# Differential attention on one core: the squares of the turned output go in front of two casts in ScalarE's order

## The chip, the cores and the metric

The kernel is one launch on one core of a Trainium2 chip. Its engines are TensorE (PE in the profile, with PEld for its weight loads), VectorE (DVE), ScalarE (ACT), GpSimd (POOL) and SyncE (SP, which here only starts DMAs). Each engine works through its own list of instructions in order, and engines wait for each other on semaphores. The metric is the device time of one execution in microseconds (us): the median of the runs.

## What is computed

One layer of a hybrid backbone for 256 prompt tokens and 2048 latent tokens. The part that the change touches is the differential attention and the norm behind it:

```python
def diff_attention(q, k, v, lam):
    ...
        s = jnp.einsum('bqhmd,bkhmd->bhmqk', qblk, k).astype(jnp.float32) * scale
        p = jax.nn.softmax(s, axis=-1)
        a = p[:, :, 0] - lam * p[:, :, 1]
        return jnp.einsum('bhqk,bkhe->bqhe', a.astype(v.dtype), v)

def merge(attn, four, subln_g, lam_init, w_out):
    b, n = attn.shape[:2]
    a = rms_norm(attn, subln_g) * (1.0 - lam_init)
    return jnp.concatenate([a.reshape(b, n, ATTN_WIDTH), four], axis=-1) @ w_out
```

There are 4 heads with 2 softmax maps each. A latent query sees 512 cached keys and 2048 latent keys, 2560 in all. The output of a head (128 wide) is normed by its own mean square: that is what the squares are for.

## The kernel before, in words

**Stages.** First the input projection with the Fourier mixing, then attention (about 518 to 1281 us of the span, from the first scores to the last squares), then the output projection and the two products of the MLP.

**A group.** Attention runs over 4 heads of 8 groups (class `Group`, g = 0 to 7) of 256 latent queries, so 32 groups. A group takes four slots, one for each half j of 128 queries and each map m. For a slot, `fill` (L1081) computes the scores in 5 PSUM banks of 512 keys (tile S), `rowmax` (L1086, VectorE) finds the largest of each bank, `comb` (L1089, VectorE) the largest of all, and `exp` (L1105, ScalarE, with the sums) writes the exponentials to P0 or P1. The 5 banks S are all that there are, so the fill of the next slot's bank b waits for this slot's exp of bank b. `combine` (L1110 to L1121, mostly GpSimd) makes P0 - lambda' P1.

**The product with V, two slots behind.** The combined map is turned by transposes on TensorE, `tr(kb)` (L1136), two key blocks at a time into a PSUM tile pt, of which there are two. `ah(kb)` (L1143, ScalarE) copies pt to SBUF, as a cast to the high part; `al(kb)` (L1148, VectorE) takes the rest, pt minus the high part. For two of the ten pairs, kb = 4 and 14, the copy is exact and there is no low part. Only after that is a pt free for the next `tr`. `mul(kb)` multiplies with V into the bank po: L95, L96 and L97 for high and low parts, L1162 for the pairs 4 and 14. Slots alternate between two pairs and three: 0 and 2; 4, 6 and 8; 10 and 12; 14, 16 and 18. I number the slots of a group's own exps 0 to 3; the transposes of pairs 10 and 12 of the group ahead stand in slot 0, those of 14, 16 and 18 in slot 1.

**The end of a group.** When a group's products are complete, `o1` (L1173) copies po columns 0 to 255 to SBUF, `o2` (L1177) turns the two halves back into columns 256 to 511 of the same bank po, `o4` (L1183) squares these on ScalarE with a sum over each row, twice 128x128, and `o5` to `o9` turn the sums to a factor on GpSimd, send it through DRAM and scale the output. There is one po. The next group's products write its columns 0 to 255 while `o2` and `o4` use the other half, and TensorE's first matmul into po behind `o4` in the program, the next group's `mul(4)` (L1162), waits for the squares.

**What sets the order.** Each step is entered with a time, `add(t, fn)`, and the whole stage is written out in order of these times (L1363 to L1365), which fixes the order on every engine. T is the length of a slot in that table and u = T / 5. The times are only keys for sorting. For the last group (`gr.last`) the steps behind `o1` are kept in a list, LASTO, and called from the output projection in the order of that list.

Of the kernel before, what the change touches and what calls it, by code (L numbers as in the profile page):

```python
# [41 lines left out]
def body(tc, a, out):  # L42
    nc = tc.nc
    ctx = ExitStack()
    with ctx:
# [944 lines left out]
        with ExitStack() as c3_:  # L990
# [289 lines left out]
            def add(t, fn, *args):  # L1280
                ev.append((t, len(ev), fn, args))
# [20 lines left out]
            for h in range(H):  # L1302
                hd, hp = Head(0, h), Head(1, h)
                base = h * 32 * T
                add(base - 18 * T + 0.7 if h else -3.04 * T, hd.load_k)
                add(base - 14 * T + 0.7 if h else 0.9 * T, hd.load_v)
                e = 4 * T * (h == H - 1)
                add(base + 2 * T - e + 0.7, hp.load_k)
                add(base + 2 * T - e + 0.71, hp.load_v)
                gp = Prompt(hp, 0)  # L1310
                G = [base + (AVS + 4 * g) * T for g in range(8)]
                add(G[1] - 3 * T - e, gp.qload)
                for j in range(2):
                    for m in range(2):
                        for t, fn in ((0.4, gp.scores), (0.85, gp.rowmax), (2.7, gp.exp)):
                            add(G[1 + 2 * j + m] - e + t * u, fn, j, m)
                    add(G[2 + 2 * j] - e + 8 * u, gp.combine, j)
                for t, fn, *args in ((0.25, gp.tr, 0), (0.9, gp.ah), (1.4, gp.al), (17.0, gp.mul), (20.85, gp.o1), (24.45, gp.oq),
                                     (25.3, gp.o2), (26.0, gp.o5), (26.05, gp.opow), (29.5, gp.o6), (34.0, gp.o7),
                                     (40.2, gp.o8), (43.0, gp.o9)):  # L1320
                    add(G[5] - e + t * u, fn, *args)
                for g in range(hd.ng):
                    gr = Group(hd, g)
                    add(base - (4 if h or g > 1 else 3) * T + 0.6 * u if base else -3.03 * T, gr.qload)
                    for st in range(4):
                        j, m = divmod(st, 2)
                        t0 = base + st * T
                        for b in range(hd.nbk):
                            add(t0 - T + (0.76 + 0.66 * b) * u, gr.fill, j, m, b)
                            add(t0 - T + (1.26 + 0.66 * b) * u, gr.rowmax, j, m, b)  # L1330
                            add(t0 + 0.66 * b * u, gr.exp, j, m, b)
                        add(t0 - 0.45 * u, gr.comb, j, m)
                        if m:
                            add(t0 + (4.5 if gr.last and j else 5.9) * u, gr.combine, j)
                            if gr.last and j:
                                add(t0 + T + 5.3 * u, gr.combine_v, j)
                    kbs = list(range(0, hd.nkt, 2))
                    for q in range(4):
                        w = base + (AVS + q) * T
                        if q % 2 == 0:  # L1340
                            order = [kbs.pop(0) for _ in range(2)]
                            tr_t, ah_t, al_t = [0.7, 2.2], [3.3, 3.8], [4.6, 5.2]
                        else:
                            order = [kbs.pop(0) for _ in range(3)]
                            tr_t, ah_t, al_t = [0.7, 2.2, 3.86], [3.3, 3.8, 4.4], [None, 4.6, 5.2]
                        for n, kb in enumerate(order):
                            add(w + tr_t[n] * u, gr.tr, kb)
                            add(w + (2.0 if gr.drain and kb == FULL[0] else ah_t[n]) * u, gr.ah, kb)
                            if al_t[n]:
                                add(w + al_t[n] * u, gr.al, kb)  # L1350
                            add(w + T + (3.9 + 0.01 * n) * u, gr.mul, kb)
                            if q == 3 and not n:
                                add(w + 3.95 * u, gr.mul_part, kb)
                    w = base + (AVS + 5) * T + 1.0 * u
                    for t, fn in ((0, gr.o1), (0.4, gr.o2), (7.85, gr.o4), (9.2, gr.o5), (11.8, gr.o6), (16.3, gr.o7), (23.4, gr.o8), (26.0, gr.o9)):
                        if gr.last and t > 1:
                            LASTO.append(fn)
                        else:
                            add(w + t * u, fn)
                    base += 4 * T  # L1360
# [357 lines left out]
        with c5r, ExitStack() as c5:  # L1718
# [157 lines left out]
            with tc.manual_schedule():  # L1876
                for n, (q, p) in enumerate(ITEMS):
# [22 lines left out]
                    fn, args = FINISH.get(n, (None, ()))  # L1900
# [66 lines left out]
        with ExitStack() as c6:  # L1967
# [62 lines left out]
            with tc.manual_schedule():  # L2030
# [41 lines left out]
                for j in range(3):  # L2072
                    t = 6 + j
# [70 lines left out]
```

## Time and profile before

| | |
|---|---|
| median of 3 runs | 2888.55 us (2887.37 to 2888.84) |
| the profiled execution | 2891.27 us |
| its span | 2889.5 us |
| TensorE busy | 2831.2 us, 98% of the span |
| ScalarE busy | 1538.7 us, 53% |
| VectorE busy | 1977.9 us, 68% |
| GpSimd busy | 1075.5 us, 37% |
| mean granted clock of TensorE | 0.998 |

A row of the timeline gives the start in us, the length, the engine, the line, what is written from what, how often (x2 for two in a row, merged), and in brackets how long the engine had been idle and whose work ended that. A row of the waits gives who waited for whom, the total in us, the number of times and the longest. A matmul row's end is modelled. ScalarE's exps and squares with a sum appear as two rows, the activation and the reading of the accumulator; a row can begin a little before the one ahead of it has ended.

### The profile page before, as it was taken

How to read it: one execution, taken by the hardware profiler on the slowest of the kernel's cores; microseconds unless marked ns; L12 is line 12 of the kernel's file. 1: busy time of each engine (PE TensorE's matmuls, PEld its weight loads, DVE VectorE, ACT ScalarE, POOL GpSimd, SP SyncE). 2: the span in 40 equal slices, each digit the busy share in tenths (PEclk: the TensorE clock that was granted, in tenths of full speed). 3: DMA queues.
4: the chain of work that ended last, by engine and by line, in shares of the span. 5: the costliest groups of instructions: out<-in, count | busy, mean ns of one | idle time of the engine just before them, and what ended most of it. 6: DMA issues, size and time to landing. Idle time of an engine off the chain costs nothing.

```text
span 2889.5 us, 42978 instructions
## 1 busy us (share of the span) xinstructions
PE 2831.2 (98%) x15029; PEld 2452.5 (85%) x15029; DVE 1977.9 (68%) x3325; ACT 1538.7 (53%) x3479; POOL 1075.5 (37%) x887
## 2 busy tenths in 40 slices
PE   8999999999999999999999999999999999999999
PEld 5888888687788888788889999999998888888887
DVE  7767786887887888864468778777775344345554
ACT  4333333788888888863356566556554332232221
POOL 1211223788898898852213333334332000000000
PEclk9999999999999999999999999999999999999999
DMA  7777767331222321337776676676656464445663
GB/s 282 222 203 206 229 203 250 150 108 47 77 74 52 110 43 43 97 74 219 235 238 223 217 245 230 220 241 223 219 192 235 148 203 151 138 143 176 206 208 110
DMA packets 404795, 497.69 MB, mean 172 GB/s; under 512 B 31539, under 2 KB 320672, under 8 KB 401506
## 3 DMA queue, kind: packets, MB, share of 16 engines
q1 hardware_dynamic: 399088, 484.35, 53.0%
q0 software_dynamic: 1936, 7.41, 0.8%
q10 hardware_dynamic: 3554, 3.17, 0.3%
q8 instruction: 119, 1.95, 0.3%
q14 instruction: 98, 0.80, 0.1%
HBM read 317.30 MB, written 179.62 MB: 172 GB/s over the span
## 4 chain that ended last, share of the span: by engine, by line
PE 54%; DVE 1%; issue 0%; ACT 0%; POOL 0%; DVEq 0%
PE ps L95 8%; PE ps L97 8%; PE ps L96 8%; PE pB L1761 2%; PE pB L1760 2%; PE pB L1759 2%; PE pA L1760 2%; PE pC L1760 2%; PE pC L1759 2%; PE pA L1759 2%; PE pA L1761 2%; PE pC L1761 2%; PE po L97 2%; PE po L96 2%; PE po L95 2%; PE pD L1761 1%
## 5 line engine op out<-in xcount | busy, mean ns | idle before, releaser
L1086 DVE TENSOR_REDUCE mxs<-Ss 128x1 f32<-128x512 f32 x636 | 405.3, 686 | 125.9 <-PE Ss L1081 118.0
L1436 DVE TENSOR_TENSOR sl<-sr,sh 128x768 fp32r<-128x768 f32 x168 | 161.8, 964 | 331.5 <-ACT sh L1435 331.1
L1121 POOL TENSOR_TENSOR P0s<-P0s,P1s 128x1024 f32<-128x1024 f32 (+2 forms) x128 | 376.7, 2943 | 10.7
L1435 ACT CAST sh<-sr 128x768 fp32r<-128x768 f32 x168 | 140.6, 838 | 418.3 <-PE ps L96 418.3
L1801 POOL TENSOR_TENSOR gs<-g,g 128x384 f32<-128x384 f32 x48 | 69.7, 1453 | 469.3 <-ACT g L1771 426.4
L1105 ACT ACTIVATE P1s<-Ss,mxs 128x512 f32<-128x512 f32 x318 | 215.4, 694 | 37.9 <-DVE mxs L1089 37.3
L95 PE MATMUL pj<-wh,hh 128*128 128x512 f32 x576 | 228.6, 397 | 2.8 <-DVE hh L556 2.0
L95 PE MATMUL ps<-thT,sh 128*128 128x512 f32 x585 | 227.6, 389 | 0.0
L96 PE MATMUL ps<-tlT,sh 128*128 128x512 f32 x585 | 227.6, 389 | 0.0
L97 PE MATMUL ps<-thT,sl 128*128 128x512 f32 x585 | 227.6, 389 | 0.0
L96 PE MATMUL pj<-wl,hh 128*128 128x512 f32 x576 | 226.8, 394 | 0.5 <-DVE wl L517 0.5
L97 PE MATMUL pj<-wh,hl 128*128 128x512 f32 x576 | 225.3, 391 | 0.0
L1105 ACT ACTIVATE P0s<-Ss,mxs 128x512 f32<-128x512 f32 x318 | 214.5, 692 | 4.9 <-DVE mxs L1089 4.0
L1136 PE MATMUL pts<-ident,P0s 128*128 128x128 f32 x1280 | 192.3, 274 | 4.4 <-DVE als L1148 1.8
L1081 PE MATMUL Ss<-KS0s,Qs 128*128 128x512 f32 x636 | 190.4, 420 | 0.4 <-ACT P1s L1105 0.4
L1081 PE MATMUL Ss<-KS1s,Qs 128*128 128x512 f32 x636 | 189.3, 422 | 1.5 <-ACT P0s L1105 1.1
L1770 ACT ACTIVATE g<-uz 128x384 f32<-128x384 f32 x144 | 75.7, 526 | 200.7 <-DVE uz L1793 174.0
L1136 PEld LDWEIGHTS pts<-ident,P0s 128*128 128x128 f32 x1280 | 152.2, 140 | 35.8 <-issue 4.6
L1143 ACT CAST ahs<-pts 128x512 fp32r<-128x512 f32 x256 | 146.4, 606 | 60.4 <-PE pts L1136 60.4
L1120 POOL TENSOR_SCALAR P1s<-P1s,tots 128x1024 f32<-128x1024 f32 (+2 forms) x128 | 172.0, 1344 | 5.7
L1148 DVE TENSOR_TENSOR als<-pts,ahs 128x512 fp32r<-128x512 f32 x256 | 163.7, 681 | 12.0 <-ACT ahs L1143 11.9
L95 PE MATMUL ps<-ophT,sh 128*128 128x512 f32 x423 | 164.7, 389 | 1.1 <-DVE uz L1793 1.1
(534 smaller groups left out, 8020.0 us busy)
## 6 DMA issues: line engine op xcount, KB each, us to landing
sr<-sd SPq DMA_DIRECT2D x84, 768.0 KB, 4.3
a<-in_w SPq DMA_DIRECT2D x184, 256.0 KB, 3.6
sd<-gs SPq DMA_DIRECT2D x192, 192.0 KB, 1.9
sd<-g SPq DMA_DIRECT2D x144, 192.0 KB, 4.2
wm<-in_w_mod SPq DMA_DIRECT2D x32, 512.0 KB, 5.3
Qs<-qd SPq DMA_DIRECT2D x32, 512.0 KB, 5.3
b<-in_w SPq DMA_DIRECT2D x64, 256.0 KB, 4.8
b<-tsum SPq DMA_DIRECT2D x64, 256.0 KB, 4.6
```

Of the source, the lines that this page charges most:

```text
L95: nc.tensor.matmul(ps, lh, rh, start=first, stop=False)
L96: nc.tensor.matmul(ps, lh, rl, start=False, stop=False)
L97: nc.tensor.matmul(ps, ll, rh, start=False, stop=last)
L1081: nc.tensor.matmul(S[:, :w], self.Q[:, x, m, j * P:j * P + P], self.hd.KS[m][:, b * 512:b * 512 + w], start=(x == 0), stop=(x == 1))
L1086: nc.vector.tensor_reduce(self.mx[j][:, m, b:b + 1], self.S[j, m, b], axis=AX.X, op=ALU.max)
L1105: nc.scalar.activation(dst, S, AF.Exp, bias=self.mx[j][:, m, 6:7], accum_out=self.sm[j][:, m, b:b + 1])
L1120: nc.gpsimd.tensor_scalar(p, p, tot[:, 3:4], 0.0, op0=ALU.mult, op1=ALU.add)
L1121: nc.gpsimd.tensor_add(d, d, p)
L1136: nc.tensor.transpose(pt[:, c:c + P], self.p0[j][:, (kb + t) * P:(kb + t + 1) * P], ident)
L1759: nc.tensor.matmul(ps, wh[:, c], hh[:, k, :], start=first and k == 0, stop=False, skip_group_check=True)
L1760: nc.tensor.matmul(ps, wh[:, c], hl[:, k, :], start=False, stop=False, skip_group_check=True)
L1761: nc.tensor.matmul(ps, wl[:, c], hh[:, k, :], start=False, stop=k == 3, skip_group_check=True)
```

## The change

One number in the table of times: `o4`, the squares, is entered 0.95 u earlier, and so sorts in front of the casts of the same slot instead of behind them.

```diff
                     w = base + (AVS + 5) * T + 1.0 * u
-                    for t, fn in ((0, gr.o1), (0.4, gr.o2), (7.85, gr.o4), (9.2, gr.o5), (11.8, gr.o6), (16.3, gr.o7), (23.4, gr.o8), (26.0, gr.o9)):
+                    for t, fn in ((0, gr.o1), (0.4, gr.o2), (6.9, gr.o4), (9.2, gr.o5), (11.8, gr.o6), (16.3, gr.o7), (23.4, gr.o8), (26.0, gr.o9)):
                         if gr.last and t > 1:
                             LASTO.append(fn)
```

ScalarE's order in slot 0 of group 3 of the first head, as a difference (osqs_0 and osss_0 are the squares and their sums of group 0, ahs_1_10 the cast of pair 10 of group 1, P0s_3_0 and P1s_3_0 the exps of group 3; a number at the end of a name counts tiles):

```order
 L1105 ACTIVATE P0s_3_0_5902,sms_3_0_5841<-Ss_3_0_0_4_5874,mxs_3_0_5840 128x512
-L1143 CAST ahs_1_10_5947<-pts_1_10_5910 128x512
-L1143 CAST ahs_1_12_5952<-pts_1_12_5936 128x512
-L1183 ACTIVATE osqs_0_5954,osss_0_5955<-po 128x128 x2
+L1183 ACTIVATE osqs_0_5946,osss_0_5947<-po 128x128 x2
+L1143 CAST ahs_1_10_5951<-pts_1_10_5910 128x512
+L1143 CAST ahs_1_12_5956<-pts_1_12_5936 128x512
 L1105 ACTIVATE P1s_3_0_0_5976,sms_3_0_5841<-Ss_3_0_1_0_5915,mxs_3_0_5840 128x512
```

The two squares now stand directly behind the last exp of map 0, and the casts of pairs 10 and 12 behind them. This happens 31 times, once for each group but the last, whose `o4` is in LASTO.

The last of the 31 places has no exps around it, since there is no further group (group 6 and 7 of the last head):

```order
 L1143 CAST ahs_7_8_14724<-pts_7_8_14707 128x512
-L1143 CAST ahs_7_10_14742<-pts_7_10_14731 128x512
-L1143 CAST ahs_7_12_14744<-pts_7_12_14737 128x512
-L1183 ACTIVATE osqs_6_14746,osss_6_14747<-po 128x128 x2
+L1183 ACTIVATE osqs_6_14742,osss_6_14743<-po 128x128 x2
+L1143 CAST ahs_7_10_14746<-pts_7_10_14731 128x512
+L1143 CAST ahs_7_12_14748<-pts_7_12_14737 128x512
 L1143 COPY ahs_7_14_14781<-pts_7_14_14770 128x512
```

Here too the squares move past two casts. On TensorE, VectorE and GpSimd no instruction changes its place. On SyncE one does, at the end of attention (att_79 is the attention output of group 6 of the last head, xo are rows of x for the residual):

```order
 L1582 DMA mT_14900<-four 128x4x128
-L1208 DMA att_79<-oTs_6_14694 128x256
 L1576 DMA xo_14903<-in_x_prompt 128x1024
 L1576 DMA xo_14905<-in_x_sample 128x1024
+L1208 DMA att_79<-oTs_6_14694 128x256
 L217 DMA g_1_14865<-gate_104 128x1024
```

The store of that output now stands behind two loads of x.

## Prediction

> **What bounds the kernel now.** I read the page first, then the table of windows, then the waits of TensorE and ScalarE alone in the steady part of attention (583 to 1275 us), then the timeline of one group, engine by engine.
>
> ```profile
> span 2889.5 us, 42978 instructions
> PE 2831.2 (98%) x15029; PEld 2452.5 (85%) x15029; DVE 1977.9 (68%) x3325; ACT 1538.7 (53%) x3479; POOL 1075.5 (37%) x887
> ```
>
> TensorE is busy 98% of the span, so only time in which it stands still is to be had from a reordering: 2889.5 - 2831.2 = 58.3 us. The windows give length, then busy us of PE, PEld, DVE, ACT and POOL, TensorE's granted clock, DMA share and GB/s, here for a piece of attention and for the last stage:
>
> ```profile
> 583.00:700.00 117.00, 112.26 (x719) 94.56 (x718) 94.64 (x187) 101.11 (x284) 103.18 (x84) 1.00 0.27 77
> 2300.00:2880.00 580.00, 580.00 (x2561) 480.41 (x2560) 279.18 (x370) 161.98 (x223) 0.00 (x0) 1.00 0.50 166
> ```
>
> In attention TensorE is idle 4.74 of 117 us, in the last stage not at all, at the same clock of 1.00. What ends its idle time in attention is one row, and the largest waits of ScalarE there are two:
>
> ```profile
> PE po L1162 <- ACT osqs L1183: 28.1, 31, 1.4
> ...
> ACT ahs L1143 <- PE pts L1136: 60.7, 91, 3.1
> ACT P1s L1105 <- DVE mxs L1089: 33.8, 56, 1.5
> ```
>
> TensorE waits 28.1 us, 31 times, for the squares; ScalarE waits 60.7 us for TensorE's transposes and 33.8 us for VectorE's row maximum. TensorE sets the pace, but for a stop once in each group. The stop itself, on TensorE:
>
> ```profile
> 605.03 1.19 PE L1081 MATMUL Ss<-KS1s,Qs 128*128 128x512 f32 x4
> 607.09 1.13 PE L1162 MATMUL po<-ahs,vf4s 128*128 128x256 f32 x4 [0.86 <-ACT osqs L1183]
> 609.45 0.60 PE L1136 MATMUL pts<-ident,P0s 128*128 128x128 f32 x4
> ...
> 611.62 1.17 PE L1081 MATMUL Ss<-KS0s,Qs 128*128 128x512 f32 x4
> 612.63 0.60 PE L1136 MATMUL pts<-ident,P0s 128*128 128x128 f32 x4
> ```
>
> and what ScalarE does in the same slot and the next:
>
> ```profile
> 605.18 0.22 ACT L1105 ACTIVATION_READ_ACCUMULATOR P0s<-Ss,mxs 128x1 f32 x1
> 605.28 1.09 ACT L1143 CAST ahs<-pts 128x512 fp32r<-128x512 f32 x2
> 606.22 0.32 ACT L1183 ACTIVATE osqs<-po 128x128 f32<-128x128 f32 x1
> ...
> 606.84 0.19 ACT L1183 ACTIVATION_READ_ACCUMULATOR osqs<-po 128x1 f32 x1
> 607.37 0.69 ACT L1105 ACTIVATE P1s<-Ss,mxs 128x512 f32<-128x512 f32 x1 [0.33 <-DVE mxs L1089]
> ...
> 610.60 0.22 ACT L1105 ACTIVATION_READ_ACCUMULATOR P1s<-Ss,mxs 128x1 f32 x1
> 610.70 0.60 ACT L1143 COPY ahs<-pts 128x512 f32<-128x512 f32 x1
> 611.90 0.59 ACT L1143 CAST ahs<-pts 128x512 fp32r<-128x512 f32 x1 [0.60 <-PE pts L1136]
> 613.27 0.59 ACT L1143 CAST ahs<-pts 128x512 fp32r<-128x512 f32 x1 [0.78 <-PE pts L1136]
> 613.88 0.69 ACT L1105 ACTIVATE P0s<-Ss,mxs 128x512 f32<-128x512 f32 x1
> ```
>
> After the last exp of map 0 ScalarE does two casts from 605.28 to 606.22, then two squares to 606.84 + 0.19 = 607.03; TensorE's product starts 0.06 us later. It had ended its scores at 605.03 + 1.19 = 606.22. Everything TensorE does later in this group, and through the casts of slot 1 the exps at 613.88, comes late by that stop.
>
> **The change part by part: the squares go first.** In front of the casts they can start at 605.28 and take the same 0.81 us (606.22 to 607.03), to 606.09; with the same 0.06 us TensorE starts at 606.15. That is 0.94 us earlier than 607.09, the length of the two casts. Would TensorE itself be ready? A slot without that wait shows how soon the product may follow the scores, and when the squares' input was there:
>
> ```profile
> 617.12 1.18 PE L1081 MATMUL Ss<-KS1s,Qs 128*128 128x512 f32 x4
> 618.14 0.82 PE L1162 MATMUL po<-ahs,vf14s 128*128 128x128 f32 x4
> 621.21 0.44 PE L1177 MATMUL po<-ident,oTs 128*128 128x128 f32 x2
> ```
>
> There the product starts 1.02 us after the scores; the same in slot 0 would be 606.05. So the squares remain the last to arrive, by 0.10 us, and the gain is 0.94 us, not 1.04. The profile's own idle, 0.86 us, is the lower of the three, since matmul ends are modelled. I take 0.94, because it is a difference of two times of the same instruction. The squares' input, the transposes L1177, comes most of a slot ahead (621.21 here, with the next squares due one slot later), so they wait for nothing in front.
>
> **The casts go 0.81 us later**, from 605.28 to 606.09, and end at 606.09 + 1.09 = 607.18. Behind them on ScalarE stand the exps of map 1, which today start at 607.37 and wait for VectorE, not for ScalarE. The sum of ScalarE's work ahead of them is unchanged, so they cost nothing. The other reader is VectorE:
>
> ```profile
> 607.11 0.16 DVE L1089 TENSOR_REDUCE mxs<-mxs 128x1 f32<-128x5 f32 x1
> 607.19 1.28 DVE L1148 TENSOR_TENSOR als<-pts,ahs 128x512 fp32r<-128x512 f32 x2
> 610.55 3.11 DVE L1086 TENSOR_REDUCE mxs<-Ss 128x1 f32<-128x512 f32 x5 [2.08 <-PE Ss L1081]
> 613.69 0.16 DVE L1089 TENSOR_REDUCE mxs<-mxs 128x1 f32<-128x5 f32 x1
> ```
>
> Its two subtractions stand behind the row maximum of 607.11 and start at 607.19 and, half of 1.28 later, about 607.8. The casts would be ready at about 606.65 and 607.18, still ahead of both. So the two pt tiles come free at the same time as today, by 608.47, and TensorE's next transposes, 609.45 today and 608.51 then, find them free. Without this cover of 0.6 us each late cast would cost what is left of 0.81.
>
> **What is late next, in slot 1.** TensorE arrives 0.94 earlier; the exps of map 1 do not. Two things there hang on these exps. The last score bank is filled in the second half of the row at 611.62, about 612.2, and is freed at 610.60 + 0.22 = 610.82: 1.4 us to spare, 0.44 after. The transposes of pair 18 (612.63) need the pt of pair 14, whose copy follows the exps and ends at 610.70 + 0.60 = 611.30. How soon transposes follow such a copy is shown by a place where they wait for one, in slot 3:
>
> ```profile
> 599.91 0.61 ACT L1143 COPY ahs<-pts 128x512 f32<-128x512 f32 x1
> ...
> 600.69 0.60 PE L1136 MATMUL pts<-ident,P0s 128*128 128x128 f32 x4
> ```
>
> 600.69 - 600.52 = 0.17. So pair 18 could go at 611.47; it will want to go at 611.69. The spare is 0.22 us. VectorE's gap of 2.08 ahead of its maxima shrinks to 1.14, ScalarE's gaps of 0.60 and 0.78 ahead of the casts to 0.44 together, and the exps of 613.88, which follow cast and row maximum (613.85) at once, move to 612.94. From there the group runs as today, 0.94 earlier. GpSimd, busy 103.18 of 117 us (88%), would be at 88 / (1 - 0.04) = 92%: still not the bound.
>
> **The last of the 31 places** has no exps:
>
> ```profile
> 1269.84 1.03 PE L1136 MATMUL pts<-ident,P0s 128*128 128x128 f32 x8
> 1270.48 1.07 ACT L1143 CAST ahs<-pts 128x512 fp32r<-128x512 f32 x2 [1.17 <-PE pts L1136]
> ...
> 1272.27 1.13 PE L1162 MATMUL po<-ahs,vf4s 128*128 128x256 f32 x4 [1.40 <-ACT osqs L1183]
> ```
>
> The squares (0.81) fit in ScalarE's idle 1.17 ahead of the casts, so the whole 1.40 us goes; between 0 (if the end of the stage hangs on something else) and 1.40 I take 1.40.
>
> **SyncE's one move** is at that end:
>
> ```profile
> 1285.24 0.33 SPq L1208 DMA_DIRECT2D att<-oTs  x1
> 1285.61 0.43 SPq L1576 DMA_DIRECT2D xo<-in_x_prompt  x1
> 1286.09 0.46 SPq L1576 DMA_DIRECT2D xo<-in_x_sample  x1
> ```
>
> The store may be issued up to 0.43 + 0.46 = 0.9 us later, the loads 0.33 earlier. The output projection reads this output only with later tiles; I price it at nothing, with 0.9 us once as its bound on either side.
>
> **The sum.** 30 x 0.94 + 1.40 = 29.6 us. The bounds of the wait removed are 28.1 (the profile's idle) and 30 x 1.04 + 1.4 = 32.6. The span becomes 2889.5 - 29.6 = 2859.9, the profiled execution 2891.27 - 29.6 = 2861.7. The median of the runs was 2888.55, 2.7 below the profiled execution; from it I forecast 2888.55 - 29.6 = 2859.0 us. In the stages behind attention TensorE is busy throughout, so they pass the gain on.
>
> **The rivals.**
>
> *Part of it is given back in slot 1.* The tightest place above is the pt of pair 14, with 0.22 us to spare. If copy and release take 0.46 us longer than I read, the gain of a group is held at 0.94 - 0.24 = 0.70, and 30 x 0.70 + 1.4 = 22.4: 2866. For it: the exps it hangs on really do not move. Against it: the spare is positive. Chance 0.12.
>
> *Nothing is gained, because the late casts hold pt.* If the pt tiles came free 0.81 us later and the transposes with them, 30 x 0.81 = 24.3 of the 29.6 would come back: 2883.3, which is 5.3 us or 0.18% under today. Against it: VectorE, not the casts, frees them, at the same time as now, and today's transposes come 0.98 after that. Chance 0.05. The Trainium skill, PSUM — Partial Sum Buffer, "Summary: rules for kernel authors", asks to evacuate PSUM promptly; by that rule a change that puts squares ahead of the copies out of pt is the wrong way round and would come out here. The trace disagrees so far: one po is what TensorE waits for, 31 times, and no wait of L1136 for these two casts is among its waits.
>
> *Slower: ScalarE changes its function table.* Exp and squares now stand side by side.
>
> ```profile
> 2.89 1.28 ACT L112 ACT_TABLE_LOAD   x1 [2.89 <-DMA rows<-in_c_ctx]
> ```
>
> A load takes 1.28 us. One ahead of the squares and one ahead of the next exps would end the squares at 607.37 instead of 607.03, and start the exps of map 1 at 607.18 + 2.56 = 609.74 instead of 607.37; pair 14 is then copied at 613.67, pair 18 turned at 613.84 instead of 612.63, 1.2 us later. 30 x 1.2 = 36: 2925 us. It decides as soon as a switch in front of the squares costs more than the 0.94 that they move. Against it: the row is the only load of the whole trace, though squares stand ahead of exps already (606.84, 607.37), and the changed program's list for ScalarE has only this one as well. Chance 0.02. The Trainium skill, ScalarE: Activation LUTs, "Table sets: the hidden batching unit", would have calls batched by set; a switch costs about 2.66 us there by its section "What ACT_TABLE_LOAD costs". By an estimate from that page two a group would be 30 x 5.3 = 160 us; the trace shows no second set in use.
>
> That the change does not do what it says is excluded by the order: the squares move past two casts at all 31 places.
>
> **How the numbers follow.** The forecast, 2859.0, has 0.81, the partial return 0.12, the return of nearly all 0.05, slower 0.02. The range runs from 2855 (32.6 gained and the store's 0.9) to 2868 (the partial return with 2 us for a place that is tighter still). About 0.2%, 5.8 us, is what a measurement of this kernel can tell from no change; so faster has 0.81 + 0.12 = 0.93, the same 0.05, slower 0.02.
>
> **What would show it.** Right: the wait of L1162 for the squares gone or under 0.2 us each; squares starting right behind an exp; casts of 10 and 12 not waited for by L1148; TensorE busy over 99% in attention, and the idle of ScalarE ahead of the casts of 16 and 18 down from 1.38 to about 0.44 us. Wrong: a new wait of L1136 for L1143 or L1148, of L1081 for L1105, a second table load, or a group that is shorter by much less than 0.94 us.

## The result and the profile after

| | before | after |
|---|---|---|
| median of 6 runs each | 2888.7 us | 2864.31 us (2861.61 to 2865.02) |
| ratio, 95% interval | | 0.9914 (0.9902 to 0.9927) |
| profiled execution | 2891.27 us | 2864.23 us |
| its span | 2889.5 us | 2862.4 us |

The kernel is 24.4 us faster; the forecast was 29.7 from this median (2859.0), with a range of 2855 to 2868. The page, and then pieces of the table of windows: one of attention, and four of 2 us each behind its end.

```profile
span 2862.4 us, 42998 instructions
PE 2829.3 (99%) x15029; PEld 2453.4 (86%) x15029; DVE 1978.0 (69%) x3325; ACT 1534.8 (54%) x3479; POOL 1075.4 (38%) x887
```

```profile
583.00:700.00 117.00, 116.40 (x746) 98.23 (x745) 97.92 (x192) 105.06 (x296) 107.46 (x86) 1.00 0.31 83
...
1256.00:1258.00 2.00, 0.00 (x0) 0.00 (x0) 0.30 (x1) 0.00 (x0) 1.66 (x3) 1.00 1.10 405
1258.00:1260.00 2.00, 0.93 (x3) 0.52 (x4) 1.90 (x3) 0.00 (x0) 1.09 (x2) 0.81 1.05 400
1260.00:1262.00 2.00, 2.00 (x5) 1.60 (x6) 2.00 (x4) 0.00 (x0) 0.00 (x0) 0.50 0.99 359
1262.00:1264.00 2.00, 2.00 (x9) 1.56 (x8) 2.00 (x4) 0.00 (x0) 0.00 (x0) 0.84 0.99 284
```

In attention TensorE is now busy 116.40 of 117 us (112.26 before), as foretold. Behind it, where the output projection begins, stands something new: TensorE idle through a whole window, then at half its granted clock. The waits name it; of the old one only weight loads are left.

```profile
PE po L95 <- DVE mh L1588: 4.4, 1, 4.4
...
PEld po L1162 <- ACT osqs L1183: 9.7, 30, 0.3
```

The same group as in the prediction, now about 3.9 us earlier: TensorE, ScalarE and VectorE.

```profile
602.15 1.17 PE L1081 MATMUL Ss<-KS1s,Qs 128*128 128x512 f32 x4
603.23 1.13 PE L1162 MATMUL po<-ahs,vf4s 128*128 128x256 f32 x4
...
608.77 0.60 PE L1136 MATMUL pts<-ident,P0s 128*128 128x128 f32 x4
```

```profile
602.39 0.30 ACT L1183 ACTIVATE osqs<-po 128x128 f32<-128x128 f32 x1
...
602.98 0.19 ACT L1183 ACTIVATION_READ_ACCUMULATOR osqs<-po 128x1 f32 x1
603.07 1.06 ACT L1143 CAST ahs<-pts 128x512 fp32r<-128x512 f32 x2
604.48 0.69 ACT L1105 ACTIVATE P1s<-Ss,mxs 128x512 f32<-128x512 f32 x1 [0.35 <-DVE mxs L1089]
...
607.81 0.60 ACT L1143 COPY ahs<-pts 128x512 f32<-128x512 f32 x1
608.28 0.62 ACT L1143 CAST ahs<-pts 128x512 fp32r<-128x512 f32 x1
609.40 0.59 ACT L1143 CAST ahs<-pts 128x512 fp32r<-128x512 f32 x1 [0.50 <-PE pts L1136]
```

```profile
604.23 0.16 DVE L1089 TENSOR_REDUCE mxs<-mxs 128x1 f32<-128x5 f32 x1
604.30 1.28 DVE L1148 TENSOR_TENSOR als<-pts,ahs 128x512 fp32r<-128x512 f32 x2
606.66 3.13 DVE L1086 TENSOR_REDUCE mxs<-Ss 128x1 f32<-128x512 f32 x5 [1.08 <-PE Ss L1081]
```

The squares end at 603.17 and the product starts 0.06 us later, 1.08 behind the scores in place of 2.06. The exps of map 1 still wait for the row maximum (0.35, before 0.33), VectorE's subtractions still follow it at once, and its gap ahead of the next maxima has shrunk from 2.08 to 1.08.

How the gain adds up is best read from one instruction that each group has once, the product L1162 of pair 4. Rows of the first group, of the thirtieth and of the last, of before and then of after (the last of before, at 1272.27, stands in the prediction):

```profile
560.96 1.02 PE L1162 MATMUL po<-ahs,vf4s 128*128 128x256 f32 x4
...
1239.56 1.13 PE L1162 MATMUL po<-ahs,vf4s 128*128 128x256 f32 x4 [0.87 <-ACT osqs L1183]
```

```profile
558.94 1.03 PE L1162 MATMUL po<-ahs,vf4s 128*128 128x256 f32 x4
...
1210.04 1.13 PE L1162 MATMUL po<-ahs,vf4s 128*128 128x256 f32 x4
...
1240.07 1.13 PE L1162 MATMUL po<-ahs,vf4s 128*128 128x256 f32 x4
```

Over 29 groups 678.60 us have become 651.10: 0.948 us a group. The last two groups take 32.71 and 30.03: 2.68 more. Attention has gained 27.5 + 2.7 = 30.2 us. (The first product stands 2.0 us earlier in this execution, ahead of anything that was changed; in the other runs it stands between 557.7 and 561, so the spans' difference of 27.1 holds that much luck.) From the last of these products to the end of the span it is 1617.2 us before (2889.5 - 1272.27) and 1622.3 after: 5.1 us were lost again behind attention. So the change is worth 30.2 - 5.1 = 25.1 us in these two executions; the medians say 24.4. Behind attention, after:

```profile
1245.44 0.73 POOL L1204 TENSOR_TENSOR oTs<-oTs,rbs 128x256 f32<-128x256 f32 x1 [7.37 <-DMA rbs<-rs]
...
1247.90 0.32 SPq L1194 DMA_DIRECT2D rs<-osss  x1
...
1251.01 0.32 SPq L1199 DMA_DIRECT2D rbs<-rs  x1
...
1251.38 0.43 SPq L1581 DMA_DIRECT2D mT<-att  x1
...
1257.70 0.69 DVE L1588 CAST mh<-mT 128x1024 fp32r<-128x1024 f32 x1 [4.71 <-DMA mT<-att]
...
1258.54 0.47 PE L95 MATMUL po<-woh,mh 128*128 128x512 f32 x1 [4.39 <-DVE mh L1588]
...
1259.78 0.80 PE L97 MATMUL po<-woh,ml 128*128 128x512 f32 x1 [0.54 <-DVE ml L1589]
1260.37 0.63 PE L95 MATMUL po<-woh,mh 128*128 128x512 f32 x1
...
1262.50 0.46 PE L97 MATMUL po<-woh,ml 128*128 128x512 f32 x1
```

and before:

```profile
1278.94 0.32 SPq L1199 DMA_DIRECT2D rbs<-rs  x1
...
1279.31 0.43 SPq L1581 DMA_DIRECT2D mT<-att  x1
...
1285.06 0.70 DVE L1588 CAST mh<-mT 128x1024 fp32r<-128x1024 f32 x1 [0.45 <-issue]
...
1285.94 0.44 PE L95 MATMUL po<-woh,mh 128*128 128x512 f32 x1
```

SyncE must load mT, the attention output for the second tile of the output projection. That load stands behind the load of the factors rb of the last group but one, which waits for the store of these factors, which waits for GpSimd, which waits for the factors of the group before it (7.37 us). This chain of two trips through DRAM came 27.9 us earlier (1279.31 to 1251.38), TensorE's last product 32.2. Before, the cast of mT ended at 1285.76 and TensorE's first product with it began at 1285.94, without a wait, but with next to nothing to spare (after, where TensorE does wait, it starts 0.15 us behind the cast). Now TensorE stands 4.39 us for it, and then six matmuls, from 1259.78 to 1262.50, take 2.72 us from start to start where six take 1.36 at the full clock: another 1.4. Against these 5.8 us TensorE's wait for the first norm of the next stage is 1.0 us shorter, which leaves 4.8 of the 5.1. The row of the waits before, and then after:

```profile
PE ptb L249 <- DVE xn L236: 1.6, 1, 1.6
...
PE ptb L249 <- DVE xn L236: 0.6, 1, 0.6
```

What meets at the end is not the gain of all groups. From the thirtieth group's product to the issue of mT it is 39.75 us before (1239.56 to 1279.31) and 41.34 after (1210.04 to 1251.38), while TensorE's way through the last two groups went from 32.71 to 30.03. The transfers had followed the gain of the first 29 groups. What TensorE is ahead of them at the end is the 2.68 us of the last two groups and the 1.59 us by which the chain itself has grown, together the 4.3 us between 32.2 and 27.9.

### The profile page after: what moved, and what is told of

It reads as the page before. It is cut to its first block, busy times and chain, and to the rows that moved or that the text cites. A ratio compares the mean times of both kernels' runs of the same rounds, so it can differ in the third digit from the quotient of the medians.

```text
span 2862.4 us, 42998 instructions
## 1 busy us (share of the span) xinstructions
PE 2829.3 (99%) x15029; PEld 2453.4 (86%) x15029; DVE 1978.0 (69%) x3325; ACT 1534.8 (54%) x3479; POOL 1075.4 (38%) x887
## 4 chain that ended last, share of the span: by engine, by line
PE 54%; DVE 1%; DMA 0%; issue 0%; ACT 0%; POOL 0%; DVEq 0%; SPq 0%
PE ps L95 8%; PE ps L96 8%; PE ps L97 8%; PE pB L1761 2%; PE pB L1759 2%; PE pB L1760 2%; PE pA L1759 2%; PE pA L1761 2%; PE pA L1760 2%; PE pC L1761 2%; PE pC L1759 2%; PE pC L1760 2%; PE po L97 2%; PE po L96 2%; PE po L95 2%; PE pD L1759 1%
## 5 line engine op out<-in xcount | busy, mean ns | idle before, releaser
L95 PE MATMUL pj<-wh,hh 128*128 128x512 f32 x576 | 228.2, 396 | 2.0 <-DVE hh L556 2.0
L95 PE MATMUL ps<-thT,sh 128*128 128x512 f32 x585 | 227.6, 389 | 0.0
L95 PE MATMUL ps<-ophT,sh 128*128 128x512 f32 x423 | 164.7, 389 | 1.1 <-DVE uz L1793 1.1
```

What stands on the lines that cost most here:

```text
L95: nc.tensor.matmul(ps, lh, rh, start=first, stop=False)
```

## The experiments

The theory: **the bank po is all that TensorE waits for in a group; each us that the squares end earlier is one us of every group, as long as they end behind the scores; what is missing of the sum is lost to SyncE's queue at the end of attention.** Rivals: that the casts' place matters by itself; that still earlier is still better; that the loss is spread or belongs to the factors' trips. Four kernels ran together on one chip, then four more, then three; each set has its own runs of the kernel before (2889.05, 2889.66 and 2888.46 us).

**The changed kernel again**, as yardstick for the first set.

> The changed kernel once more, as the yardstick for the others of this set. Both theories: about 2864 us, 24 to 25 under the kernel before (2888.7). The trace should again show attention shorter by about 30 us and a wait of TensorE of about 4.4 us for the load of the second tile of the output projection.

Measured: 2863.63 us, ratio 0.9908 (0.9894 to 0.9921); the wait for mT is 4.7 us.

**Squares from SBUF, ScalarE's order as before.**

```diff
-                        nc.scalar.activation(osq, self.po[:, 256 + j * P:256 + j * P + P], AF.Square, accum_out=self.oss[:, j:j + 1])
+                        nc.scalar.activation(osq, self.oT[:, j * P:j * P + P], AF.Square, accum_out=self.oss[:, j:j + 1])
```

> The kernel before with ScalarE's order untouched, but the squares read the output from SBUF, before it is turned, and no longer from the bank po (so the mean squares are of the wrong axis and the outputs are not the reference's; the amount of work is the same). Theory (TensorE waits for the bank po, and nothing else about the squares' place matters): L1162 no longer waits, attention is shorter by 28 to 33 us, the total about 2864 us or, with the same loss at the handover, up to 3 us to either side. Rival (the place of the casts behind the squares is what paces the slot): no gain, 2887 to 2889 us.

Measured: 2861.64 us, 27.4 under the kernel before (ratio 0.9900, 0.9887 to 0.9914). With the casts still ahead of the squares, the whole stop is gone: a group is 1.12 us shorter (1203.90 - 557.89 for the 29 groups). The casts' place by itself is worth nothing; the bank is the cause. It also shows the size of the stop, 1.12 us: the squares of the changed kernel, at 0.95, are still the last to arrive, by 0.17.

**Squares between the casts.**

```diff
-                    for t, fn in (..., (6.9, gr.o4), ...):
+                    for t, fn in (..., (7.5, gr.o4), ...):
```

> The changed kernel with the squares between the two casts (7.5 in the table): one cast ahead of them instead of none or both. Theory (each us that the squares end earlier is one us of TensorE in every group, as long as they end behind the scores): 0.47 us a group less than the kernel before, 29 groups 13.6 us and up to 2.7 us in the two last ones, so attention shorter by 14 to 16.5 us, the handover still nearly unharmed: about 2874 us (2871 to 2876). Rival (there is a threshold, and either most of the 0.95 comes with the first cast or nothing does): near 2864 or near 2888 us.

Measured: 2875.44 us, ratio 0.9949 (0.9934 to 0.9963), 14.2 us faster; 0.476 us a group, where one cast is 0.47. Half the move, half the gain; no threshold. What is left of the wait:

```profile
PE po L1162 <- ACT osqs L1183: 13.0, 31, 0.9
```

**Squares ahead of the last exp.**

```diff
-                    for t, fn in (..., (6.9, gr.o4), ...):
+                    for t, fn in (..., (6.5, gr.o4), ...):
```

> The changed kernel with the squares one place further ahead still, between the fourth and the fifth exp of map 0 (6.5 in the table). Theory (from there on the exps and the scores that follow them are what TensorE waits for): the fifth exp ends 0.81 us later, the last score bank is filled about 0.65 us later than in the changed kernel, and with it the row maximum and the exps of map 1; against that the product behind the scores gains at most the 0.1 to 0.2 us that the squares were still last. 0.5 to 0.7 us a group lost against the changed kernel: about 2880 us (2877 to 2884). Rival (still earlier is still better, ScalarE's sum being the same): 2860 to 2864 us.

Measured: 2877.08 us (ratio 0.9955, 0.9938 to 0.9971), 12.6 us under the kernel before in place of 24.4; a group gains only 0.49 us in place of 0.95. The wait has gone over to the score banks:

```profile
PE Ss L1081 <- ACT P0s L1105: 11.7, 31, 1.1
```

So the place that was chosen is the best in this row: one step later and one step earlier each lose half.

This run also shows what sets the loss at the end. Its groups gain half as much, and yet TensorE waits as long for mT as in the changed kernel:

```profile
PE po L95 <- DVE mh L1588: 4.7, 1, 4.7
```

With the squares between the casts, where the gain of a group is nearly the same, that wait is 1.2 us. What differs is the last two groups, from product to product: 30.05 us here, 30.03 in the changed kernel, 31.90 with the squares between the casts.

**Casts later still.**

```diff
+                    for j in range(2):
+                        nc.scalar.activation(osq, self.oT[:, j * P:j * P + P], AF.Square, accum_out=self.oss[:, 2 + j:3 + j])
```

> The changed kernel with two more squares (of data in SBUF, into a place that is overwritten later) behind the two of the output and ahead of the casts: the casts and the exps of map 1 come about 0.8 us later, while the bank po is free as early as in the changed kernel. Theory (0.35 us of wait for the row maximum and 0.2 to 0.4 us in the bank of pair 14 and the last score bank are spare, the rest counts): 0.1 to 0.3 us a group lost, 3 to 9 us, 2867 to 2873 us. Rival 1 (VectorE and the tiles pt hang on these casts, so that each us of delay counts): 24 us lost, about 2888. Rival 2 (ScalarE has 0.8 us to spare): 2863 to 2865 us.

Measured: 2871.01 us (ratio 0.9933, 0.9918 to 0.9948); 0.78 us a group in place of 0.95, so 0.17 lost of some 0.8 us of delay. The cover that the prediction gave to the late casts is there, but at about twice the delay it no longer holds for all of it. Rival 1, by which each us counts, is out.

**mT loaded by way of ScalarE**, in the changed kernel and in the kernel before.

```diff
-                nc.sync.dma_start(mT[:, 0:4, :], att[i // 2][:, c:c + P].rearrange("(k p) t -> p k t", p=P))
-                nc.sync.dma_start(mT[:, 4:8, :], four[:, i * P:i * P + P].rearrange("(k p) t -> p k t", p=P))
+                q = nc.scalar if i == seq[1] else nc.sync
+                q.dma_start(mT[:, 0:4, :], att[i // 2][:, c:c + P].rearrange("(k p) t -> p k t", p=P))
+                q.dma_start(mT[:, 4:8, :], four[:, i * P:i * P + P].rearrange("(k p) t -> p k t", p=P))
```

> The changed kernel, but the two loads of mT for the second tile of the output projection are issued by ScalarE instead of SyncE, where they stood behind the load of the factors rb, which waits for a store. Theory (the missing 5 us of the sum were lost at the end of attention, to this load and to the lower clock behind the wait): the wait of 4.4 us goes, the nine matmuls of 0.63 us become 0.39, so 5 to 6 us less than the changed kernel, about 2858.5 us. Rival (the handover is bound by the factors' round trip through DRAM anyway, or the loss is spread): within 1.5 us of the changed kernel, about 2864 us.

> The kernel before, with the same loads issued by ScalarE. Theory: in the kernel before the load came 0.5 us late at most, so nothing or up to 1 us is to be had: 2887.5 to 2889 us. Rival (the load's queue is worth 5 us in any kernel, and has nothing to do with the change): about 2883 us.

Measured: 2860.00 us on the changed kernel (ratio to the kernel before 0.9896, 0.9880 to 0.9911), 3.6 under it, and 2887.64 on the kernel before, ratio 0.9993 (0.9984 to 1.0002), not to be told from no change. The times alone do not settle that the load's queue matters only behind the change, as the theory has it: the second interval reaches 4.6 us. The waits do: that of L95 for the cast of mT is not there in the kernel before, is 4.4 us in the changed kernel, and is gone here, where the load is issued at 1242.92. But 5 to 6 us were expected. Another wait has grown, from 0.6 to 2.9 us, and the granted clock falls to 0.50 with this one too:

```profile
1242.92 0.39 ACTq L1582 DMA_DIRECT2D mT<-att  x1
...
1272.87 1.97 PE L249 MATMUL ptb<-ident,xn 128*128 128x128 f32 x8 [2.94 <-DVE xn L236]
```

**The factors' transfers by way of GpSimd.**

```diff
-                    return nc.gpsimd if self.last else nc.sync, self.hd.tok0 // 2 + self.g
+                    return nc.gpsimd if self.last or self.drain else nc.sync, self.hd.tok0 // 2 + self.g
```

> The changed kernel with the three small transfers of the last group but one (factors out, factors in, output out) issued by GpSimd, as those of the last group are, so that on SyncE nothing stands ahead of the loads of the output projection. Theory (the 5 us lost at the handover are SyncE's queue standing behind the factors' round trip): the waits of TensorE for mT (4.4 to 4.7 us) and, unlike with ScalarE issuing mT alone, for xn stay away: 5 to 7 us less than the changed kernel, 2857 to 2859 us. Rival (the round trip itself bounds the handover, by way of the last outputs): 2862 to 2864 us.

Measured: 2865.86 us (ratio 0.9915, 0.9901 to 0.9930): no gain, and above what either side expected. mT comes in time here too, and so does everything else on SyncE. But the factors' store now goes out among these loads, and GpSimd stands for it:

```profile
1249.94 0.66 POOL L1194 DMA_DIRECT2D rs<-osss  x1 [0.29 <-POOL osss L92]
...
1256.72 0.55 POOL L1199 DMA_DIRECT2D rbs<-rs  x1 [6.12 <-DMA rs<-osss]
...
1263.74 1.26 POOL L1204 TENSOR_TENSOR oTs<-oTs,rbs 128x256 f32<-128x256 f32 x1 [6.47 <-DMA rbs<-rs]
...
1277.89 0.58 POOL L92 TENSOR_TENSOR nrsb<-nssb,mhalf 128x1 f32<-128x1 f32 x1
...
1279.31 1.97 PE L249 MATMUL ptb<-ident,xn 128*128 128x128 f32 x8 [6.41 <-DVE xn L236]
```

The last row but one is the power of the next stage's first norm. It is in GpSimd's queue behind the factors of the last two groups, and TensorE waits 6.41 us for what comes of it. So my account of the handover was half of it: there are two queues that stand behind the factors' trips, SyncE's with mT and GpSimd's with the first norm, and to free one brings out the other. The rival (the trips themselves) is right for the second.

**One instruction for the squares, the sum on VectorE**, alone and with mT by way of ScalarE.

```diff
                 def o4(self):
                     ...
+                    if not self.last:
+                        ...
+                        nc.scalar.activation(self.osq, self.po[:, 256:512].rearrange("p (j e) -> p j e", j=2), AF.Square)
+                        return
                     ...
                 def o5(self):
+                    if not self.last:
+                        nc.vector.tensor_reduce(self.oss[:, 0:2], self.osq, axis=AX.X, op=ALU.add)
```

> The changed kernel with the squares as one instruction of 128x256 without a sum, and the two sums by a reduction on VectorE (in all groups but the last; a padding of 128 bytes in SBUF is left out to make room). ScalarE's squares take about 0.45 us in place of 0.81. Theory (the squares are still the last to free po, by 0.17 us a group as the kernel with squares from SBUF shows, and the end of attention then waits longer for mT): 0.17 us a group, 4.9 us, of which 1 to 2 us come back at the handover: 2860 to 2862 us. Rival (the squares are no longer last, or VectorE's extra 0.3 us a group counts): 2863 to 2866 us.

> The same, with the two loads of mT for the second tile of the output projection issued by ScalarE as well. Theory (the two gains lie in different places and add, but for the wait for xn that took the place of the one for mT): 2860 from the kernel with that load alone, less 3.5 to 5 us: 2855 to 2857 us. Rival (the round trips of the factors through GpSimd bound the handover, so that what comes earlier in attention is waited for there): 2859 to 2861 us.

> The changed kernel with only the padding of 128 bytes left out, as a yardstick for the two others. Both theories: within 1.5 us of the changed kernel, 2862 to 2865 us; if not, the others are to be read against this one.

Measured: 2860.58 us alone (ratio to the kernel before 0.9903, 0.9889 to 0.9918), and 2865.85 for its yardstick, the changed kernel without the padding (0.9919, 0.9904 to 0.9934), a little above its expected range. A group gains 1.08 us, 0.15 more than the yardstick's 0.93, so the squares were indeed the last by that much. The wait for mT grows to 6.4 us. With mT by way of ScalarE it is 2860.08 us (ratio 0.9902, 0.9886 to 0.9919), not the 2855 to 2857 of the theory; attention is as short (1.09 us a group), but

```profile
PE ptb L249 <- DVE xn L236: 3.7, 1, 3.7
```

the wait at the norm has grown from 2.9 us. That is the rival's direction, but only 0.8 of the 4.2 us by which attention is shorter than with mT alone (677.05 in place of 681.26 us from the first of the products L1162 to the last). The medians show no gain over that kernel, the profiled execution, the fastest of its four, shows 2.6 us; with a spread from 2857.95 to 2861.47 this stays open. Each against the changed kernel of its own set (for this one that without the padding), the kernel with mT alone gains 3.6 us and this one 5.8; a version that moves GpSimd's power out of that queue was not run.

## Why the prediction was right or wrong, step by step

- *The squares go first: 0.94 us a group.* Right: 0.948, and by the right cause, as the squares from SBUF show. That the squares remain last was right too, but by 0.17 us, not 0.10: besides the start, 0.06 later, the first product itself takes 1.13 us in place of the 1.03 that it takes with the squares from SBUF. The limit is 1.12, not 1.04.
- *The casts cost nothing.* Right: VectorE's subtractions start at once behind the maximum, with no new wait, and when the casts were delayed by about as much again (and the exps behind them with them) 0.17 us a group was lost.
- *Slot 1 has 0.22 us to spare.* Right: pair 14's copy ends at 608.41, pair 18 is turned at 608.77, and 0.17 of that is the way from one to the other. ScalarE's idle ahead of its casts fell to 0.50 us (0.44 forecast).
- *The last place: 1.40 us.* Too small: the last two groups together gave 2.68 where 0.94 + 1.40 were in the sum.
- *The rival by which the late casts hold pt*: refuted here. The casts are 0.7 us later within their slot, measured from the exps, and the tiles pt come free when they did, at the end of VectorE's subtractions. With it falls the rival's reading of the Trainium skill's rule to evacuate PSUM promptly (PSUM — Partial Sum Buffer, "Summary: rules for kernel authors"): what had to be read first here is the bank that TensorE waits for. *The rival with a table load*: no second load.
- *SyncE's one move at nothing, and "in the stages behind attention TensorE is busy throughout, so they pass the gain on".* This is the step that failed: 5.1 us in the traces. I priced the store that changes its place, which nobody waits for, and not what else is on that queue: the load of mT, which came just in time before, and whose chain behind the thirtieth group does not shorten with TensorE's last two groups. Nor was TensorE busy throughout there before: it waited 1.6 us for the next stage's norm. The sum, 30.2 in attention for the 29.6 forecast, is right without this term; the forecast of 2859.0 was 5.3 us too low, most of it because of this term. That 2864.3 lies within the range is in part luck: the range's upper end was made for a loss in slot 1, which did not come.

## What to carry to other kernels

When a stop in a repeated stage goes, look at the stage's end: ask there, for each queue, which transfers hang on the last turns by a chain that does not get shorter, and how much they had to spare. Here that was nothing, and the shorter last two turns were enough to make them late. Before an order on one engine is changed, follow who holds the resource that the busiest engine waits for: an accumulator bank in use by a small reader can matter more than the larger copies behind it. And a place in an order is best tried one step to either side; here each step away lost half.

## What the runs showed of the hardware

The stops of 0.86 to 1.40 us ahead of L1162 left TensorE's granted clock at 1.00. The stop of 4.39 us did not: the clock was still 1.00 at 1256 to 1258, 0.81 in the next 2 us, 0.50 in the two after, and 0.84 in the last window. In this run it falls when the work has already come back (1258.54), so that the price of a stop of 4.4 us is 5.8.

Neither the length of a stop nor its end settles when the clock falls; windows of 0.2 and 0.4 us show it. At the start of attention in the kernel before, a stop of 1.36 us that ended at 543.91 was followed by 0.50 from about 544.4 to 548, though 1.40 us at 1272 changed nothing. At the end of attention, in the changed kernel and the ten others with a stop of 1.9 us or more there, the clock fell 2.2 to 5.1 us after the last matmul's end and came back 2.8 to 5.9 us after the work did. In the changed kernel without the padding, where TensorE stands 4.68 us at the same place, it fell at 1256.8, before the work came back at 1259.14. It stayed low for about 3.4 us (here 1259.2 to 1262.6) in five of these eleven runs, for about twice that in five, and for 10.2 us in one. So the same stop can cost a us more or less, and a difference of that size between two of these kernels need not have another cause.

The Trainium skill, TensorE: Matmul & The Clock Gate, Part 1 on the HAM clock gate, describes a gate that halves the clock some time after the last matmul (5.2 us in the run that it shows) and opens again after about 3.4 us of work. The halving agrees with these windows and 5.2 us is near the latest fall; the return, 2.8 to 5.9 us after the work's, agrees with 3.4 us only roughly.

A small store that another queue waits for took 3.1 us from its issue by SyncE to the next step (1247.90 to 1251.01) while the DMA engines were nearly idle (share 0.02). Issued by GpSimd, with the factors' transfers on that engine, it took 3.8 us when they were idle (1267.19 to 1271.00, share 0.01) and 6.8 us (1249.94 to 1256.72) when loads of some hundred KB had just been issued beside it. So the longer time goes with the traffic, not with the engine that issues.
